# Strassen block products in the down projections of a SwiGLU trunk, with sums of weights on VectorE

## The chip, the cores and the metric

The kernel runs on one core of one Trainium2 chip. Its time is the device time of one execution in microseconds (us), the median of several runs. The engines of a core are TensorE (PE, with its weight loads shown apart as PEld), VectorE (DVE), ScalarE (ACT), GpSimd (POOL) and SyncE (SP, which here issues most DMAs).

## The reference

Two layers of a decoder over a sequence of 256 tokens, width 1024, all in float32. Each layer is a half-step SwiGLU with layer norm, three token mixers side by side with a combined input and an output projection, layer norm, and a second half-step SwiGLU with layer norm. The change concerns the four SwiGLUs (two in each layer):

```python
D_MODEL, SEQ, DEPTH, D_FF = 1024, 256, 2, 2816

def swiglu(x, w_gu, w_down):
    gate, up = jnp.split(x @ w_gu, 2, axis=-1)
    return (jax.nn.silu(gate) * up) @ w_down

def hybrid_layer(x, ...):
    h = layer_norm(DEEPNORM_ALPHA * x + 0.5 * swiglu(x, ffn1_w_gu, ffn1_w_down), ...)
    ...                     # DeltaNet, sliding-window attention, memory attention, merge
    h = layer_norm(DEEPNORM_ALPHA * h + merged @ w_out, ...)
    return layer_norm(DEEPNORM_ALPHA * h + 0.5 * swiglu(h, ffn2_w_gu, ffn2_w_down), ...)
```

A down projection is the product of a 256 x 2816 hidden matrix with a 2816 x 1024 weight matrix.

## The kernel before

**Weights.** All weights come as one stream, `wst`, in tiles of 128x1024 float32 (512 KB), called units here. `unit` does for each: SP's DMA into `raw` (pool `praw`, four buffers), a cast on ACT to a float32r tile `whi` (pool `phi`, five buffers), and on DVE `wlo = raw - whi` (pool `plo`, five buffers; `split` is these two). A `raw` buffer is free when that subtraction is done. Every product is then three matmuls (`mm3`): high part by high part, high by low, low by high, each of 512 columns into a PSUM bank. `newest` is the last split made.

**The gate and up phase.** Hidden tiles come in groups i = 0 to 10, each of four units and 48 matmuls. `out` takes silu times up, transposes on DVE, and sends the result through DRAM with POOL's DMAs (tiles `tr` and `pt`). `settle` splits what came back into `u{i}`, which holds two hidden tiles of 128 rows (by 256 tokens), high and low; it is put off so that the round trip has time, the last two to within the down projection (after units 2 and 10; the table `along`).

**The down projection** is `projA`, called at the end of `Ffn.rest`: NFT = 22 units (unit uu is the weights' row block uu). For a unit there are four blocks: tb = 0, 1 (halves of the tokens) by j = 0, 1 (halves of the 1024 output columns), each an `mm3` into one of four `acc` banks, 12 matmuls a unit. The first two units (`lead`) run with one half of the tokens and then the other. The last units (`tail`, 4 in a layer's first SwiGLU, 6 in its second) are kept to the end and run block by block, so that the residual addition and layer norm of a finished half (`Post`) stand beside the products of the other. The last block of all goes into two half banks (`ends`, from the `at` banks): `Post.early` takes its bank `d` out of the way as soon as the units ahead of the tail are in it.

**Order.** A scheduler sets the order of each engine's instructions from priorities: a unit's load, cast and subtraction get a priority AHEAD = 300 steps earlier than their place in the program. The order is fixed when the kernel is built; each engine works through its own row in that order and waits by semaphores for the others. PSUM has four `acc` banks, two `sm` and two `at`; in the down projection `sm` and `at` are idle before the tail.

Of the kernel before, what the change touches and what calls it, by code (L numbers as in the profile page):

```python
# [17 lines left out]
P = 128  # L18
# [20 lines left out]
def tile_trunk(ctx, tc, x, xT, mem, memT_, wst, lnp, memln, cvw, rows, cst, out):  # L39
# [64 lines left out]
    def unit(w=U, dst=None, cuts=1, behind=None, parts=1):  # L104
# [17 lines left out]
        return hi, lo  # L122

    def split(hi, lo, src):
        return nc.scalar.copy(hi, src).ins, nc.vector.tensor_tensor(lo, src, hi.bitcast(F32), op=ALU.subtract).ins  # L125
# [54 lines left out]

    def projA(xt, w, kpu, nk, outs, tail=0, dsts=(), lead=0, after=None, behind=None, held=(), led=None, along=None, ends=(), units=None):

        def one(k, kk, hi, lo, tb, j):
            ts = slice(tb * P, (tb + 1) * P)
            n = [o.shape[-1] for o in outs[tb]]
            first = k == ((nu - tail) * kpu if tb and j and ends and len(outs[1]) > 2 else 0)
            c = kk * w + sum(n[:j])
            c = slice(c, c + n[j])
            mm3(outs[tb][j], (xt[0](k)[:, ts], xt[1](k)[:, ts]), (hi[:, c], lo[:, c]), first, k == nk - 1 or bool(ends and tb and j and k == (nu - tail) * kpu - 1))

        nu = nk // kpu
        units = units or {}

        def get(uu):
# [34 lines left out]
    def full_rows():  # L229

        a, b, c, d = (acc() for _ in range(4))
        return [[a, b], [c, d]], [at()[:, 0:S] for _ in range(2)]

# [75 lines left out]
    class Ffn:  # L309
        def __init__(self, before=None):  # L310
            self.units = []
            for q in range(KD // 2):
                if before:
                    before(q)
                self.units.append(unit(cuts=2 if before and q == 0 else 1, parts=2 if before and q in (1, 2) else 1))
            self.hu, self.bank, self.due = {}, {}, []

# [29 lines left out]
        def out(self, i, banks):  # L347
# [9 lines left out]
            if len(self.due) > 1:  # L357
                self.settle(act, ins)
            y = T(p2, [P, D], "pt")[:, 0:512]
            d = T(pd, [4, 32, 4, P], "tr")  # L360
# [3 lines left out]
            self.last = act, ins, back  # L364
            self.due.append((i, y))

        def settle(self, act, vec):

            if self.due:
                i, y = self.due.pop(0)  # L370
                hi, lo = (self.h(i)[:, n].rearrange("p a (t q s) -> p (a t) q s", t=2, q=4) for n in range(2))
                with tc.issue_after(act), tc.issue_after(vec):
                    split(hi, lo, y.rearrange("p (q n s) -> p n q s", q=4, n=4))

        def rest(self, hT, tail, dsts, post, mid={}, behind=None, more={}):
            for i in range(1, NFT // 2):
                banks = [acc() for _ in range(2)]
# [14 lines left out]
            outs, ends = full_rows()  # L392
            projA((lambda k: self.hu[k // 2][:, 0, k % 2, :], lambda k: self.hu[k // 2][:, 1, k % 2, :]), D, 1, NFT, outs, tail, dsts, 2, post, along={2: self.settle, 10: self.settle, **more}, ends=ends)

# [809 lines left out]
```

## Time and profile before

| | us |
|---|---|
| median of 3 runs | 1275.11 (1274.64 to 1275.47) |
| span of the profiled execution | 1272.1 |
| down projection, layer 0, first SwiGLU | 126.25 to 183.71, and 2.8 of half-bank matmuls |
| down projection, layer 0, second SwiGLU | 574.04 to about 630 |
| down projection, layer 1, first SwiGLU | 756.24 to about 814 |
| down projection, layer 1, second SwiGLU | 1203.51 to about 1260 |

In the profile's rows the columns are the start (in rows of time), the length in us, the engine, the line, the operation, out<-in, and in square brackets how long the engine sat idle before and what released it. In grouped rows the mean of one is in ns. "SPq" is SP's queue, by which weights are loaded. The times of a DMA are from issue to landing.

### The profile page before, as it was taken

How to read it: one execution, taken by the hardware profiler on the slowest of the kernel's cores; microseconds unless marked ns; L12 is line 12 of the kernel's file. 1: busy time of each engine (PE TensorE's matmuls, PEld its weight loads, DVE VectorE, ACT ScalarE, POOL GpSimd, SP SyncE). 2: the span in 40 equal slices, each digit the busy share in tenths (PEclk: the TensorE clock that was granted, in tenths of full speed). 3: DMA queues.
4: the chain of work that ended last, by engine and by line, in shares of the span. 5: the costliest groups of instructions: out<-in, count | busy, mean ns of one | idle time of the engine just before them, and what ended most of it. 6: DMA issues, size and time to landing. Idle time of an engine off the chain costs nothing.

```text
span 1272.1 us, 18768 instructions
## 1 busy us (share of the span) xinstructions
PE 1260.6 (99%) x6948; PEld 1073.3 (84%) x6948; DVE 864.1 (68%) x1274; ACT 661.4 (52%) x982; POOL 207.2 (16%) x365
## 2 busy tenths in 40 slices
PE   9999999999999999999999999999999999999997
PEld 6888889999778888888888888899987788888886
DVE  6678576886647776665766665759867387766565
ACT  6456444655664544454454554456556554454441
POOL 1232000002311102221012220000023101122100
PEclk9999999999999999999999999999999999999999
DMA  8988765655534748877668877566463356577762
GB/s 294 317 271 289 248 208 159 211 171 129 172 117 144 241 141 259 241 241 220 217 210 244 256 252 219 177 185 213 150 167 134 100 189 225 174 246 244 241 220 82
DMA packets 77643, 261.40 MB, mean 205 GB/s; under 512 B 11920, under 2 KB 13328, under 8 KB 77552
## 3 DMA queue, kind: packets, MB, share of 16 engines
q1 hardware_dynamic: 66320, 232.40, 56.0%
q0 software_dynamic: 11088, 27.68, 8.1%
q8 instruction: 54, 0.88, 0.3%
q14 instruction: 37, 0.30, 0.1%
q10 hardware_dynamic: 144, 0.13, 0.0%
HBM read 246.40 MB, written 13.76 MB: 205 GB/s over the span
## 4 chain that ended last, share of the span: by engine, by line
PE 89%; DMA 3%; POOL 3%; DVE 2%; issue 2%; ACT 0%; SPq 0%; DVEq 0%; POOLq 0%; ACTq 0%
PE acc L134 80%; PE at L134 3%; PE sm L134 2%; DMA w<-dr 2%; PE sm L137 2%; DVE wlo L125 1%; DMA raw<-in_wst_dram 1%; POOL t L808 1%; POOL t L807 1%; PE acc L332 1%; PE acc L333 1%; POOL l L798 1%; PE acc L335 1%; DMA dr<-t 1%; ACT whi L125 0%
## 5 line engine op out<-in xcount | busy, mean ns | idle before, releaser
L125 DVE TENSOR_TENSOR wlo<-raw,whi 128x1024 fp32r<-128x1024 f32 (+2 forms) x405 | 487.0, 1210 | 279.7 <-ACT whi L125 277.5
L125 ACT CAST whi<-raw 128x1024 fp32r<-128x1024 f32 (+2 forms) x405 | 413.7, 1029 | 400.6 <-PE acc L134 316.2
L134 PE MATMUL acc<-whi,hT 128*128 128x512 f32 (+1 forms) x1824 | 562.2, 386 | 0.5 <-ACT whi L125 0.5
L134 PEld LDWEIGHTS acc<-whi,hT 128*128 128x128 f32 x1824 | 340.0, 188 | 69.8 <-ACT whi L125 2.3
L134 PE MATMUL acc<-wlo,hT 128*128 128x512 f32 (+1 forms) x912 | 350.2, 384 | 0.0
L134 PE MATMUL acc<-whi,u 128*128 128x512 f32 x812 | 259.5, 392 | 0.0
L134 PEld LDWEIGHTS acc<-wlo,hT 128*128 128x128 f32 x912 | 171.3, 188 | 33.1 <-DVE wlo L125 1.0
L134 PEld LDWEIGHTS acc<-whi,u 128*128 128x128 f32 x812 | 152.3, 188 | 32.1 <-DVE u L125 0.5
L134 PE MATMUL acc<-wlo,u 128*128 128x512 f32 x406 | 158.2, 390 | 0.0
L362 POOL DMA_DIRECT2D tr<-t x176 | 96.3, 554 | 311.6 <-DVE t L356 303.5
L134 PE MATMUL acc<-hT,whi 128*128 128x256 f32 x672 | 122.2, 284 | 0.0
L134 PEld LDWEIGHTS acc<-hT,whi 128*128 128x128 f32 x672 | 104.6, 192 | 0.0
L134 PE MATMUL acc<-hT,wlo 128*128 128x256 f32 x336 | 95.0, 283 | 0.0
L134 PEld LDWEIGHTS acc<-wlo,u 128*128 128x128 f32 x406 | 76.3, 188 | 15.4
L134 PEld LDWEIGHTS acc<-hT,wlo 128*128 128x128 f32 x336 | 64.3, 191 | 0.0
L363 POOL DMA_DIRECT2D pt<-tr x44 | 25.0, 569 | 192.5 <-DMA tr<-t 138.4
L353 ACT ACTIVATE t<-acc 128x256 f32<-128x256 f32 x88 | 33.5, 381 | 36.9 <-PE acc L134 36.9
L134 PE MATMUL acc<-u,u 128*128 128x512 f32 x186 | 46.4, 394 | 0.0
L354 DVE TENSOR_TENSOR t<-t,acc 128x256 f32<-128x256 f32 x88 | 36.6, 417 | 8.1 <-ACT t L353 4.1
L1000 POOL TENSOR_TENSOR u<-u,gt 128x512 f32<-128x512 f32 x16 | 20.7, 1294 | 125.0 <-DVE gt L998 125.0
L134 PEld LDWEIGHTS acc<-u,u 128*128 128x128 f32 x186 | 34.6, 188 | 7.5
L125 DVE TENSOR_TENSOR u<-pt,u 128x512 fp32r<-128x512 f32 x44 | 28.9, 657 | 9.4 <-ACT u L125 9.4
(236 smaller groups left out, 1165.0 us busy)
## 6 DMA issues: line engine op xcount, KB each, us to landing
raw<-in_wst_dram SPq DMA_DIRECT2D x409, 512.0 KB, 4.4
tr<-t POOLq DMA_DIRECT2D x176, 64.0 KB, 3.8
pt<-tr POOLq DMA_DIRECT2D x44, 256.0 KB, 5.0
raw<-in_wst_dram SPq DMA_DIRECT2D x16, 324.0 KB, 3.0
gB<-in_lnp_dram SPq DMA_DIRECT2D x6, 512.0 KB, 5.8
bB<-in_lnp_dram SPq DMA_DIRECT2D x6, 512.0 KB, 6.2
w<-dr POOLq DMA_DIRECT2D x4, 512.0 KB, 12.0
t<-in_xT_dram SPq DMA_DIRECT2D x4, 256.0 KB, 5.2
```

The lines of the kernel that those rows point to most:

```text
L125: return nc.scalar.copy(hi, src).ins, nc.vector.tensor_tensor(lo, src, hi.bitcast(F32), op=ALU.subtract).ins
L134: return pe(nc.tensor.matmul(*a, **k))
L137: return pe(nc.tensor.transpose(*a))
L332: nc.tensor.matmul(ps, hT[0][:, k, ts], hi[:, c], start=k == 0, stop=False)
L333: nc.tensor.matmul(ps, hT[0][:, k, ts], lo[:, c], start=False, stop=False)
L335: nc.tensor.matmul(ps, hT[1][:, k, ts], hi[:, c], start=False, stop=k == KD - 1)
L353: act = nc.scalar.activation(t[:, :, tb, :], g, AF.Silu).ins
L354: ins = nc.vector.tensor_tensor(t[:, :, tb, :], t[:, :, tb, :], u, op=ALU.mult).ins
L362: nc.gpsimd.dma_start(d[:, :, q].rearrange("b c x -> c b x"), z[32 * q:32 * q + 32].rearrange("c (b x) -> c b x", b=4))
L363: back = nc.gpsimd.dma_start(y, d.rearrange("b c q x -> (b c) (q x)")).ins
L798: nc.gpsimd.tensor_tensor(L32[q, c], AK[c][q, :, 0, q], cs[q, C_LV:C_LV + 32].unsqueeze(1).to_broadcast([32, 4, 32]), op=ALU.mult)
L1000: nc.gpsimd.tensor_tensor(mg[tb][:, js], mg[tb][:, js], gt[tb][:, js], op=ALU.add)
```

## The change

In the down projections every second pair of units becomes a pair by Strassen's scheme (Winograd's variant): a pair of weight tiles is a 2 x 2 block matrix of 128x512 blocks (unit uu gives b11 and b12, unit uu+1 gives b21 and b22), the two hidden tiles by two halves of tokens another. Seven block products replace eight. The pairs begin at units 4, 8, 12, 16 in a layer's first SwiGLU and at 4, 8, 12 in its second.

- `pair_unit` loads two tiles, forms on DVE the float32 sums of weights t3 = b22 − b12, t1 = b12 − b11 (over b12), t2 = t3 + b11, and t4 = b21 − t2 (over b21), and splits eight blocks of 512 columns as seven operands: both tiles (128x1024 each), t2 and t3 together (into one tile `hT` with one buffer), and t4 (into the same tile).
- `settle` forms for the second tile of `pt` the sums of the hidden tiles, four of 128x128, and splits them into a tile out of `homes` (`u13`, `u12`, `u11`, `gt`).
- `Ffn.__call__` issues the seven products, 21 matmuls. Four of them go into banks of their own (`sm`, `at`, `sm`, `at`), which stay open from the first pair to the last; three go straight to `acc` banks.
- `fold` adds the four banks to the residual after the last pair: one copy on ACT and seven operations of 128x512 on DVE.
- `ends` is allocated only after the fold, since its `at` banks are in use until then; bank d closes with the last plain unit ahead of the tail.

```diff
+    def pair_unit():
+        raw = [T(praw, [P, U], "raw") for _ in range(2)]
+        with tc.high_priority(offset=AHEAD):
+            for r in raw:
+                nc.sync.dma_start(r, wst[pos[0]:pos[0] + P * U].rearrange("(p w) -> p w", p=P))
+                pos[0] += P * U
+            (b11, b12), (b21, b22) = ((r[:, 0:512], r[:, 512:U]) for r in raw)
+            sums = T(p2, [P, U], "gt")
+            t2, t3 = sums[:, 0:512], sums[:, 512:U]
+            nc.vector.tensor_tensor(t3, b22, b12, op=ALU.subtract)
+            nc.vector.tensor_tensor(b12, b12, b11, op=ALU.subtract)
+            nc.vector.tensor_tensor(t2, t3, b11, op=ALU.add)
+            parts = [(T(phi, [P, U], "whi", F32R), T(plo, [P, U], "wlo", F32R)) for _ in range(2)]
+            for (hi, lo), r in zip(parts, raw):
+                split(hi, lo, r)
+            nc.vector.tensor_tensor(b21, b21, t2, op=ALU.subtract)
+            more = T(pu, [P, 2, 3, 512], "hT", F32R)
+            flat = more.rearrange("p n m c -> p n (m c)")
+            split(flat[:, 0, 0:U], flat[:, 1, 0:U], sums)
+            newest[:] = split(more[:, 0, 2], more[:, 1, 2], b21)
...
         for uu in range(lead, nu - tail):
-            for tb in range(2):
-                run([uu], tb, range(len(outs[tb])))
+            if uu in pairs:
+                fast(uu, outs)
+            elif uu - 1 not in pairs:
+                for tb in range(2):
+                    run([uu], tb, range(len(outs[tb])))
...
         if ends:
             after.early(outs[1].pop())
-            outs[1] += ends
+            outs[1] += ends()
...
         def settle(self, act, vec):
...
+                    if 2 * i in self.sums:
+                        s = self.sums[2 * i] = T(*self.sums[2 * i])
+                        v = z.rearrange("p (m q s) -> p m q s", m=4, q=4)
+                        for m, a, b, op in ((0, y[:, 1], y[:, 3], ALU.add), (2, y[:, 0], y[:, 1], ALU.subtract), (1, v[:, 0], y[:, 0], ALU.subtract), (3, y[:, 2], v[:, 1], ALU.subtract)):
+                            nc.vector.tensor_tensor(v[:, m], a, b, op=op)
+                        split(s[:, 0], s[:, 1], z.rearrange("p (m t) -> p m t", m=4))
...
+        def __call__(self, uu, outs):
+            if uu == self.pairs[0]:
+                self.side = [sm(), at(), sm(), at()]
+            w = pair_unit()
...
+            p1, p5, p6, p7 = self.side
+            for o, x, name in ((p1, plain(0, 0), "b11"), (p5, summed(0), "t1"), (outs[0][0], plain(1, 0), "b21"), (outs[0][1], summed(3), "b22"),
+                               (p6, summed(1), "t2"), (p7, summed(2), "t3"), (outs[1][0], plain(1, 1), "t4")):
+                own = o in self.side
+                mm3(o, x, w[name], own and first, own and last)
+            if last:
+                self.fold(p1, p5, p6, p7)
+
+        def fold(self, p1, p5, p6, p7):
+            def add(tb, j, v):
+                y = hres[tb][:, j * 512:j * 512 + 512]
+                nc.vector.scalar_tensor_tensor(y, v, 0.5 / ALPHA, y, op0=ALU.mult, op1=ALU.add)
+            u, v = (T(p2, [P, 512], "t2", bufs=4) for _ in range(2))
+            nc.scalar.copy(u, p1)
+            add(0, 0, p1)
+            nc.vector.tensor_tensor(u, u, p6, op=ALU.add)
+            nc.vector.tensor_tensor(v, u, p5, op=ALU.add)
+            nc.vector.tensor_tensor(u, u, p7, op=ALU.add)
+            add(0, 1, v)
+            nc.vector.tensor_tensor(v, u, p5, op=ALU.add)
+            add(1, 0, u)
+            add(1, 1, v)
```

How the order moves. In the rows `wlo` is the low part of a unit, `u10` the last settled hidden tile; numbers are buffers and tiles. First DVE in the middle of layer 0's first down projection. Before, one subtraction for each unit:

```order
L125 TENSOR_TENSOR wlo_263_1346<-raw_261_1344,whi_262_1345 128x1024
L125 TENSOR_TENSOR wlo_266_1364<-raw_264_1362,whi_265_1363 128x1024
L125 TENSOR_TENSOR wlo_269_1384<-raw_267_1382,whi_268_1383 128x1024
L125 TENSOR_TENSOR wlo_272_1402<-raw_270_1400,whi_271_1401 128x1024
L125 TENSOR_TENSOR u10_273_1418<-pt_231_1200,u10_273_1418 128x512
```

After, one round there: the pair of units 12 and 13 (`raw_287`, `raw_288`), then plain unit 14 (`raw_295`) with the split of t4 behind it, then plain unit 15 (`raw_298`):

```order
L134 TENSOR_TENSOR gt_289_1487<-raw_288_1484,raw_287_1483 128x512
L135 TENSOR_TENSOR raw_287_1483<-raw_287_1483 128x512
L136 TENSOR_TENSOR gt_289_1487<-gt_289_1487,raw_287_1483 128x512
L150 TENSOR_TENSOR wlo_291_1492<-raw_287_1483,whi_290_1491 128x1024
L150 TENSOR_TENSOR wlo_293_1494<-raw_288_1484,whi_292_1493 128x1024
L150 TENSOR_TENSOR hT_294_1500<-gt_289_1487,hT_294_1500 128x1024
L140 TENSOR_TENSOR raw_288_1484<-raw_288_1484,gt_289_1487 128x512
L150 TENSOR_TENSOR wlo_297_1528<-raw_295_1526,whi_296_1527 128x1024
L150 TENSOR_TENSOR hT_294_1500<-raw_288_1484,hT_294_1500 128x512
L150 TENSOR_TENSOR wlo_300_1546<-raw_298_1544,whi_299_1545 128x1024
```

Six operations of sums and sums' splits have come between the units' subtractions, and the load of the second tile of the next pair waits for unit 14's (`wlo_297`), which stands eighth. The second down projection of layer 0, after the change, DVE again (a pair, `raw_1069` and `raw_1070`, and the plain unit behind it, `raw_1077`):

```order
L134 TENSOR_TENSOR gt_1071_5794<-raw_1070_5791,raw_1069_5790 128x512
L135 TENSOR_TENSOR raw_1069_5790<-raw_1069_5790 128x512
L136 TENSOR_TENSOR gt_1071_5794<-gt_1071_5794,raw_1069_5790 128x512
L150 TENSOR_TENSOR wlo_1073_5799<-raw_1069_5790,whi_1072_5798 128x1024
L150 TENSOR_TENSOR wlo_1075_5801<-raw_1070_5791,whi_1074_5800 128x1024
L150 TENSOR_TENSOR wlo_1079_5835<-raw_1077_5833,whi_1078_5834 128x1024
L140 TENSOR_TENSOR raw_1070_5791<-raw_1070_5791,gt_1071_5794 128x512
L150 TENSOR_TENSOR hT_1076_5807<-gt_1071_5794,hT_1076_5807 128x1024
L150 TENSOR_TENSOR hT_1076_5807<-raw_1070_5791,hT_1076_5807 128x512
```

Here the plain unit's subtraction comes sixth, ahead of t4 and of the two splits into `hT`. Last the end of layer 0's first down projection on DVE. Before (`h0`, `h1` are the residual's halves; `wlo_329` and on belong to the next stage):

```order
L125 TENSOR_TENSOR wlo_306_1567<-raw_304_1565,whi_305_1566 128x1024
L125 TENSOR_TENSOR wlo_329_1712<-raw_327_1710,whi_328_1711 128x1024
L125 TENSOR_TENSOR wlo_332_1742<-raw_330_1740,whi_331_1741 128x1024
L406 SCALAR_TENSOR_TENSOR h1_222<-acc_236_1210,h1_222 128x512
L125 TENSOR_TENSOR wlo_335_1772<-raw_333_1770,whi_334_1771 128x1024
L418 SCALAR_TENSOR_TENSOR h0_221<-acc_233_1207,h0_221 128x512
```

After (`wlo_322` is the last unit's, `at_255` is p5, `at_257` is p7, `t2_309` and `t2_310` are the fold's u and v, and `wlo_347` and on belong to the next stage):

```order
L150 TENSOR_TENSOR wlo_322_1636<-raw_320_1634,whi_321_1635 128x1024
L445 TENSOR_TENSOR t2_309_1605<-t2_309_1605,at_257_1317 128x512
L438 SCALAR_TENSOR_TENSOR h0_221<-t2_310_1606,h0_221 128x512
L150 TENSOR_TENSOR wlo_347_1783<-raw_345_1781,whi_346_1782 128x1024
L150 TENSOR_TENSOR wlo_350_1813<-raw_348_1811,whi_349_1812 128x1024
L150 TENSOR_TENSOR wlo_353_1843<-raw_351_1841,whi_352_1842 128x1024
L447 TENSOR_TENSOR t2_310_1606<-t2_309_1605,at_255_1315 128x512
L438 SCALAR_TENSOR_TENSOR h1_222<-t2_309_1605,h1_222 128x512
L438 SCALAR_TENSOR_TENSOR h1_222<-t2_310_1606,h1_222 128x512
L496 SCALAR_TENSOR_TENSOR h0_221<-acc_237_1235,h0_221 128x512
```

The last reads of the side banks and the last additions to the residual stand behind three subtractions of the next stage, and the norm's first addition (L496) behind those.

More of the change, by code (lines that the diff above doesn't have):

```diff
@@ L179, in halves, with projA @@
             use(i, b)
-    def projA(xt, w, kpu, nk, outs, tail=0, dsts=(), lead=0, after=None, behind=None, held=(), led=None, along=None, ends=(), units=None):
+    def projA(xt, w, kpu, nk, outs, tail=0, dsts=(), lead=0, after=None, behind=None, held=(), led=None, along=None, ends=None, units=None, fast=None):
         def one(k, kk, hi, lo, tb, j):
@@ L188, in one @@
             c = slice(c, c + n[j])
-            mm3(outs[tb][j], (xt[0](k)[:, ts], xt[1](k)[:, ts]), (hi[:, c], lo[:, c]), first, k == nk - 1 or bool(ends and tb and j and k == (nu - tail) * kpu - 1))
+            mm3(outs[tb][j], (xt[0](k)[:, ts], xt[1](k)[:, ts]), (hi[:, c], lo[:, c]), first, k == nk - 1 or bool(ends and tb and j and k == closing))
         nu = nk // kpu
         units = units or {}
+        pairs = fast.pairs if fast else ()
+        closing = max(u for u in range(nu - tail) if u not in pairs and u - 1 not in pairs) * kpu + kpu - 1
         def get(uu):
@@ L231, in full_rows @@
         a, b, c, d = (acc() for _ in range(4))
[L232 removed]
+        return [[a, b], [c, d]], lambda: [at()[:, 0:S] for _ in range(2)]
     def together(f):
@@ new lines, in pairs @@
+        @property
+        def pairs(self):
+            return tuple(self.sums)
+        def __call__(self, uu, outs):
+            if uu == self.pairs[0]:
+                self.side = [sm(), at(), sm(), at()]
+            w = pair_unit()
+            first, last = uu == self.pairs[0], uu == self.pairs[-1]
+            h, s = self.hu[uu // 2], self.sums[uu]
+            plain = lambda a, t: tuple(h[:, n, a, t * P:(t + 1) * P] for n in range(2))
+            summed = lambda m: tuple(s[:, n, m] for n in range(2))
+            p1, p5, p6, p7 = self.side
[5 more added lines that the diff above has]
+                self.fold(p1, p5, p6, p7)
@@ L375, in rest @@
         def rest(self, hT, tail, dsts, post, mid={}, behind=None, more={}):
+            homes = ((pu, [P, 2, 4, P], "u13", F32R), (pu, [P, 2, 4, P], "u12", F32R), (pu, [P, 2, 4, P], "u11", F32R), (p2, [P, 2, 4, P], "gt", F32R))
+            self.sums = {u: home for u, home in zip(range(4, NFT - tail - 1, 4), homes)}
             for i in range(1, NFT // 2):
```

17 lines of the change are left out of this document (11 added, 6 removed).

## Prediction

> **What bounds the kernel.** I read the page's first rows and the chain by engine, then the four stretches in which the down projections run, and then what a weight tile costs on its way.
>
> ```profile
> PE 1260.6 (99%) x6948; PEld 1073.3 (84%) x6948; DVE 864.1 (68%) x1274; ACT 661.4 (52%) x982; POOL 207.2 (16%) x365
> PE 89%; DMA 3%; POOL 3%; DVE 2%; issue 2%; ACT 0%; SPq 0%; DVEq 0%; POOLq 0%; ACTq 0%
> ```
>
> TensorE is busy for 99% of the span and carries 89% of the chain. By that, each matmul taken away is a gain of its pace, as long as the weights come in time. Over the four down stages the windows say (columns: stretch, its length, busy time of each engine, clock, share of the DMA engines, GB/s):
>
> ```profile
> core 0: us, PE busy (x) PEld busy (x) DVE busy (x) ACT busy (x) POOL busy (x), PEclk, DMA share, GB/s
> 126.25:183.71 57.46, 57.46 (x255) 47.46 (x254) 33.63 (x37) 27.03 (x30) 3.83 (x7) 1.00 0.77 254
> 574.30:630.10 55.80, 55.80 (x248) 46.13 (x247) 34.27 (x40) 25.47 (x28) 2.75 (x5) 1.00 0.74 241
> 756.50:813.70 57.20, 57.20 (x254) 47.23 (x253) 33.18 (x36) 25.67 (x28) 2.75 (x5) 1.00 0.73 234
> 1203.80:1259.60 55.80, 55.80 (x248) 46.14 (x247) 30.67 (x37) 22.21 (x25) 2.97 (x6) 1.00 0.52 175
> ```
>
> In all four PE has not one gap. VectorE (DVE) has some 22 us free in each: that is the cover for the sums, as a total. Whether it is free at the right moment is the question. The pace of a matmul comes from the longest unbroken piece of the chain:
>
> ```profile
> 1094.88 164.68 PE acc L134 x726
> ```
>
> 164.68 / 726 = 0.2268 us. A plain unit (one weight tile, 12 matmuls) is 2.72 us of PE, two units 5.44; a pair of 21 matmuls is 4.76.
>
> How a tile comes in (ScalarE casts, VectorE subtracts, then the tile's `raw` buffer is free and SP sends the next load):
>
> ```profile
> SPq L115 <- DVE wlo L125: 35.4, 16, 4.9
> raw<-in_wst_dram SPq DMA_DIRECT2D x21, 512.0 KB, 4.4
> DMA to landing us min/median/max: 3.9/4.4/6.4
> 140.05 1.05 ACT L125 CAST whi<-raw 128x1024 fp32r<-128x1024 f32 x1 [1.67 <-PE acc L134]
> 142.77 1.05 ACT L125 CAST whi<-raw 128x1024 fp32r<-128x1024 f32 x1 [1.67 <-PE acc L134]
> 141.13 1.23 DVE L125 TENSOR_TENSOR wlo<-raw,whi 128x1024 fp32r<-128x1024 f32 x1 [1.49 <-ACT whi L125]
> 1211.00 3.48 DVE L125 TENSOR_TENSOR wlo<-raw,whi 128x1024 fp32r<-128x1024 f32 x3
> ```
>
> The first row is SP's waits from 128 to 183 us: of 21 loads 16 wait for a subtraction on VectorE, 35.4 us together. So the load of a tile isn't sent ahead at leisure, it is sent when VectorE frees one of the four buffers. Before, that is harmless: landing 4.4 + cast 1.05 + subtraction 1.23 = 6.7 us, and a buffer comes round every 4 × 2.72 = 10.9 us; the casts at 140.05 and 142.77 follow PE's pace and wait for PE.
>
> **The change part by part.**
>
> *Matmuls removed.* 4 pairs in each first FFN and 3 in each second make 14 over two layers, three matmuls less in each: 42 × 0.2268 = **−9.5 us**, if nothing is late.
>
> *Sums on VectorE.* A pair adds four sums of 128x512, the split of t2|t3 (128x1024) and of t4 (128x512); the fold at the end adds seven operations of 128x512.
>
> ```profile
> L500 DVE TENSOR_TENSOR pp<-pp,gB 128x512 f32<-128x512 f32 x4 | 2.8, 692 | 0.1
> L125 DVE TENSOR_TENSOR u<-pt,u 128x512 fp32r<-128x512 f32 x44 | 28.9, 657 | 9.4 <-ACT u L125 9.4
> L125 ACT CAST u<-pt 128x512 fp32r<-128x512 f32 x44 | 27.0, 614 | 11.8 <-DMA pt<-tr 11.8
> L418 DVE SCALAR_TENSOR_TENSOR h<-acc,h 128x512 f32<-128x512 f32 x18 | 12.4, 688 | 13.0 <-PE acc L134 13.0
> L852 DVE TENSOR_TENSOR w<-w,sm 128x128 f32<-128x128 f32 x4 | 1.1, 280 | 1.0 <-PE sm L134 1.0
> ```
>
> 4 × 0.69 + 1.23 + 0.66 = 4.65 us of VectorE a pair, 7 × 0.69 = 4.8 for the fold. In the first down stage that is 33.6 + 4 × 4.65 + 4.8 = 57.0 busy us, against 57.46 − 12 × 0.2268 = 54.7 that PE would need. VectorE alone is over PE there. In the second FFN it is 34.3 + 3 × 4.65 + 4.8 = 53.1 against 55.8 − 9 × 0.2268 = 53.8, just under. ScalarE gets 1.05 + 0.61 a pair and has 30 us free, so it costs nothing while VectorE is the slower. The sums of hidden tiles (for each pair four of 128x128 at 0.28 and a split of 0.66, 1.8 us) stand mostly in the gate and up phase; I take them as hidden by VectorE's idle third there.
>
> *The ring of loads in the first FFNs.* In VectorE's order a pair's eight operations and the next plain unit's subtraction stand in a row, and the load of the next pair's second tile waits for that subtraction. From the landing of the second tile: t3 and t1 1.31 (operations in a row overlap by some 0.07, as the row of three subtractions shows), cast 1.05 (t1 overwrites b12, so it must come first), three subtractions 3.48, t4 0.62, the plain one 1.23, in all 7.7 us; then the next landing. With 4.4 that is a round of 12.1, with the shortest 3.9 one of 11.6. Fewer loads stand in flight at once when the ring is late, so I take 4.1: 11.8. PE needs 4.76 + 5.44 = 10.2 for the round. Each pair after the first makes PE wait **1.6 us**.
>
> The first pair has its own: VectorE comes to it after u9 is settled (its round trip through DRAM lands then).
>
> ```profile
> 126.25 0.39 PE L134 MATMUL acc<-whi,u 128*128 128x512 f32 x1
> 131.65 0.62 ACT L125 CAST u<-pt 128x512 fp32r<-128x512 f32 x1 [3.36 <-DMA pt<-tr]
> 132.30 0.69 DVE L125 TENSOR_TENSOR u<-pt,u 128x512 fp32r<-128x512 f32 x1 [3.22 <-ACT u L125]
> 756.24 0.39 PE L134 MATMUL acc<-whi,u 128*128 128x512 f32 x1
> 759.36 0.62 ACT L125 CAST u<-pt 128x512 fp32r<-128x512 f32 x1 [1.07 <-DMA pt<-tr]
> ```
>
> In layer 0 u9 is done 6.7 us after the stage began; a hidden sum, t3, the split of u8's sums, t1, t2, three subtractions, t4, the plain one, t4's split (0.28 + 0.69 + 0.66 + 1.38 + 0.36 left of the cast + 3.48 + 0.62 + 1.23 + 0.66 = 9.4, less 0.3 for overlaps) end at 15.8. The last two matmuls of the pair read that split, so it ends at 16.3; PE without a wait would end it at 10.9 + 4.76 = 15.65: 0.7 us of wait. In layer 1 u9 comes 2.3 us sooner and nothing waits; the slack left there takes 0.3 off the next pair. Layer 0: 0.7 + 3 × 1.6 = 5.5; layer 1: 1.3 + 2 × 1.6 = 4.5. Together **+10.0**.
>
> *The end of the first FFNs.* Unit 21's load waits for unit 18's subtraction, 7.7 us after the last pair's landing; landed and cast it is ready at 7.7 + 4.1 + 1.05 = 12.9. The pair ends some 8.5 after its landing (t4's split at 8.3 comes last), and PE has 14 matmuls, 3.2 us, before it reads unit 21: a wait of 1.2. Then the half banks of the last block wait for the fold's last read of p5, behind three splits of the next stage: 0.35 more. 1.55 in each of two, **+3.1** (bounds: 0, if the ring isn't late, and 3.9 each, with the longest landing of 6.4).
>
> *Layer norm behind it.*
>
> ```profile
> 183.71 2.83 PE at L134 x24
> 186.54 0.55 PE sm L137 x4
> 187.75 6.39 PE acc L134 x54
> 194.15 0.59 PE sm L137 x4
> 185.64 1.40 DVE L296 SCALAR_TENSOR_TENSOR h<-h,rstd,bB 128x512 f32<-128x512 f32 x2
> ```
>
> PE turns to the first row half's transposes at 186.54, less than 1 us after VectorE began the last operation of that norm (185.64), and to the second half's at 194.15: little slack in each. The residual is now complete only after the fold (4.8 us) and three 1.23 us splits that the order puts ahead of its last additions. Walking it through, the first transposes wait 1.2 us, the second 2.6. Bounds 0 to 3.8; I take 3.0, nearer the upper end since those VectorE operations have nothing beside them that could be left out. **+6.0** for two.
>
> *The second FFNs.* There the plain unit's subtraction stands ahead of t4 and of the two splits, so the next load is asked for 1.31 + 1.05 + 2.4 + 1.23 = 6.0 us after a landing; 6.0 + 4.1 = 10.1 against 10.2: no wait. The settled tiles come early enough:
>
> ```profile
> 574.04 0.39 PE L134 MATMUL acc<-whi,u 128*128 128x512 f32 x1
> 576.83 0.62 ACT L125 CAST u<-pt 128x512 fp32r<-128x512 f32 x1 [0.75 <-DMA pt<-tr]
> ```
>
> 0, with bounds from 0 to 2 us a pair, which a landing of 6.4 instead of 4.1 would give. With six tail units behind the last pair, the fold has 12 × 6 × 0.2268 = 16 us of PE over it.
>
> *Sum:* −9.5 + 10.0 + 3.1 + 6.0 = **+9.6 us**, a span of 1272.1 + 9.6 = 1281.7. The median of the runs, 1275.1, is 3.0 above this span; so about **1285 us**.
>
> **The landing time, by another source.** Eight of the waits (six pairs, two of unit 21) scale with the load's way. The chain has loads that landed faster than the median:
>
> ```profile
> 389.87 3.66 DMA raw<-in_wst_dram
> 1019.32 3.45 DMA raw<-in_wst_dram
> ```
>
> [...]
>
> **The rivals.**
>
> 1. *The loads land sooner.* The ring late means fewer transfers at a time. With 3.45 the eight waits lose 0.65 each, 5.2: +4.4, so 1279.5. Against it: in the first stage no load took under 3.9.
>
> 2. *Only the ring is late.* The tail's and the norm's waits (9.1 us) are covered, since VectorE after a late ring has less left to do and the next stage's splits may be ready early: +0.5, so 1275.6, no change. For it: those terms come from my walk along an order, not from a row.
>
> 3. *All hidden: faster.* The full −9.5, 1265.6 us. One mechanism decides: whether the next pair's second tile is asked for early enough. The round must be at most 10.2, that is 7.7 us of work cut to 6.1 at a 4.1 us landing, or a landing within 2.5. It could come from VectorE operations of 128x512 that overlap more than the rows show, or from casts that run beside the sums. For it: TensorE's 89% of the chain, and 22 us of free VectorE. Against it: 57.0 us of VectorE work against 54.7 of PE.
>
> 4. *The second FFNs are late too.* The margin there is 0.1 us a round. Longer landings add up to 2 us for each of six pairs, less what the first pairs have in hand: some +10, so 1295.
>
> That the change doesn't do what it says is no rival: its order has 42 matmuls fewer on PE.
>
> **How the numbers follow.** The forecast 0.42; rival 1, 0.14; rival 2, 0.16; rival 3, 0.18; rival 4, 0.10. A measurement of this kernel can tell about 0.2%, 2.6 us, from no change: below 1272.5 is faster (rival 3: 0.18), up to 1277.7 the same (rival 2: 0.16), the rest slower (0.66). The range leaves out most of rival 3 and the far part of rival 4: 1268 to 1297. The likeliest case alone has 1281 to 1290, by the bounds of its tail and norm terms.
>
> **What would show it.** In the profile after: PE's busy time falls by about 9.5 us and yet its share of the first FFNs' down stages falls below 90%; PE's idle there is put down to the subtraction of whi or to its cast, once for each pair from the second on, 1 to 2 us each, with a round of some 11.8 us between the pairs' first products; SP's loads wait for VectorE's subtraction of the plain unit; the stretch of the second FFNs has PE without gaps. After the first FFNs' last blocks PE's transposes wait for the norm. If instead the rounds there are 10.2 us, the ring's term is wrong and rival 3 holds; if the rounds are long and the norm on time, rival 2; if the second FFNs show gaps at their pairs, rival 4.

## The result, and the profile after

The changed kernel takes 1291.63 us (median of 4 runs, 1288.22 to 1296.06) where the kernel before takes 1274.99: a ratio of 1.013, 95% interval 1.0108 to 1.0153. It is slower, by 16.6 us; the forecast was 10 us slower, with 1291.63 inside its range. The profiled execution has a span of 1290.7, 18.6 over the one before; the stretches below are those of this one execution.

The page's busy times and the chain by engine, of the changed kernel:

```profile
PE 1264.1 (98%) x6906; PEld 1067.0 (83%) x6906; DVE 957.4 (74%) x1460; ACT 688.7 (53%) x1028; POOL 206.8 (16%) x365
PE 76%; DVE 10%; DMA 8%; issue 3%; ACT 2%; POOL 0%; DVEq 0%; SPq 0%; ACTq 0%; POOLq 0%
```

PE has 42 matmuls fewer and is busy 3.5 us longer; its part of the chain fell from 89% to 76%, and VectorE and the DMAs have 18% of it where they had 5%. (The length of one matmul in the records, 0.39 us, is more than the pace of 0.227, so a gap in PE shows some 0.17 too short, and PE counts as busy while its clock is at half: 3.41 of 3.41 us from 642.40 on, at 0.50.) The four down stages, each from its first down product to its first half-bank product (columns as in the prediction):

```profile
127.05:188.43 61.38, 58.02 (x242) 44.26 (x240) 48.80 (x62) 32.75 (x39) 3.80 (x7) 1.00 0.62 211
581.52:636.74 55.22, 54.40 (x238) 44.40 (x237) 48.93 (x60) 29.79 (x35) 2.88 (x6) 1.00 0.74 233
766.46:827.77 61.31, 57.92 (x242) 44.27 (x240) 48.65 (x61) 31.30 (x37) 2.74 (x5) 1.00 0.57 183
1222.43:1277.95 55.52, 54.47 (x239) 44.31 (x238) 48.01 (x63) 27.02 (x32) 3.28 (x6) 1.00 0.56 177
```

Before, the same stretches took 57.30, 55.88, 57.30 and 55.88 us with PE without a gap. VectorE is not full in the first: 48.8 of 61.4 us. Where PE waited, in all:

```profile
PE sm L159 <- DVE wlo L150: 4.8, 8, 0.8
PE sm L162 <- DVE h L326: 3.8, 2, 1.9
PE acc L159 <- DVE t L384: 1.9, 2, 1.1
PE sm L162 <- issue: 1.8, 1, 1.8
...
PE acc L159 <- DVE hT L150: 1.2, 7, 0.2
```

First row: eight pairs of the first FFNs wait for their first subtraction. Second and fourth: the norms (the fourth, put down to issue, is PE's wait at 206.49 for layer 0's first norm, whose last operation on VectorE had begun at 205.63). Third: the first units of the second FFNs, which no step of the prediction has. From PE's starts in the two timelines, stage by stage (us against before, forecast beside it):

| stretch | forecast | measured |
|---|---|---|
| up to the first down stage | 0 | +0.8 |
| first FFN's down stage, layers 0 and 1 | +4.0, +3.0 | +4.1, +4.0 |
| from there to the second FFN's down stage | +3.35, +3.35 | +2.6, +4.7 |
| second FFN's down stage, layers 0 and 1 | −2.0, −2.0 | −0.7, −0.4 |
| from layer 0's to layer 1's first down stage | 0 | +3.4 |
| sum | +9.6 | +18.6 |

The ring of loads in the first FFN, as the chain tells one round of it (pieces under 0.05 us left out), and the t3 of the round before, from VectorE's timeline:

```profile
164.91 0.69 DVE raw L140
165.59 1.15 DVE wlo L150
166.76 3.73 DMA raw<-in_wst_dram
...
170.58 0.70 DVE gt L134
171.31 0.70 DVE raw L135
...
172.08 1.06 ACT whi L150
173.16 2.36 DVE wlo L150 x2
```
```profile
158.92 0.69 DVE L134 TENSOR_TENSOR gt<-raw,raw 128x512 f32<-128x512 f32 x1 [1.20 <-DMA raw<-in_wst_dram]
```

The chain's pieces are t4, the plain unit's subtraction, the load that it lets go (3.73 us), t3, t1, the cast and the subtractions. The round before began with t3 at 158.92, this one at 170.58: 11.66 us, forecast 11.8. The request in between left at 166.76, 7.84 us after t3 began.

Layer 0's second norm, in the chain, VectorE's and PE's timelines, and windows around it:

```profile
633.56 6.45 DMA bB<-in_lnp_dram
```
```profile
640.12 1.42 DVE L326 SCALAR_TENSOR_TENSOR h<-h,rstd,bB 128x512 f32<-128x512 f32 x2 [1.44 <-DMA bB<-in_lnp_dram]
640.93 0.66 PE L162 MATMUL sm<-cs,h 128*128 128x128 f32 x4 [1.89 <-DVE h L326]
```
```profile
636.00:641.90 5.90, 4.01 (x30) 3.63 (x29) 4.32 (x11) 0.57 (x2) 0.00 (x0) 1.00 0.39 142
641.90:645.30 3.40, 3.40 (x21) 3.40 (x19) 2.87 (x8) 1.49 (x3) 0.00 (x0) 0.57 0.00 0
```

The norm's bias row left SP's queue at 633.56, behind six weight loads of the next stage that wait for VectorE, and landed at 640.0; VectorE was ready 1.44 us before. PE waited 1.89 us, and the granted clock then averaged 0.57 over the last window (0.50 from 642.40 to 645.81 us, as the last section shows): some 1.7 us more.

### The profile page after: what moved, and what is told of

It reads as the page before. It is cut to its first block, busy times and chain, and to the rows that moved or that the text cites. A ratio compares the mean times of both kernels' runs of the same rounds, so it can differ in the third digit from the quotient of the medians.

```text
span 1290.7 us, 18905 instructions
## 1 busy us (share of the span) xinstructions
PE 1264.1 (98%) x6906; PEld 1067.0 (83%) x6906; DVE 957.4 (74%) x1460; ACT 688.7 (53%) x1028; POOL 206.8 (16%) x365
## 4 chain that ended last, share of the span: by engine, by line
PE 76%; DVE 10%; DMA 8%; issue 3%; ACT 2%; POOL 0%; DVEq 0%; SPq 0%; ACTq 0%; POOLq 0%
PE acc L159 65%; DMA raw<-in_wst_dram 5%; DVE wlo L150 5%; PE at L159 4%; PE sm L159 3%; ACT whi L150 2%; PE sm L162 1%; DMA pt<-tr 1%; DMA tr<-t 1%; PE acc L362 1%; PE acc L363 1%; PE acc L365 1%; PE at L162 1%; DVE u L150 1%; DVE hT L150 1%
## 5 line engine op out<-in xcount | busy, mean ns | idle before, releaser
L159 PE MATMUL acc<-whi,u 128*128 128x512 f32 x640 | 212.3, 394 | 1.9 <-DVE t L384 1.9
L159 PEld LDWEIGHTS acc<-whi,u 128*128 128x128 f32 x640 | 120.0, 188 | 29.4 <-issue 2.7
L159 PE MATMUL acc<-wlo,u 128*128 128x512 f32 x320 | 125.1, 391 | 0.0
L159 PEld LDWEIGHTS acc<-wlo,u 128*128 128x128 f32 x320 | 60.1, 188 | 12.9 <-DVE wlo L150 0.7
L150 DVE TENSOR_TENSOR u<-pt,u 128x512 fp32r<-128x512 f32 x56 | 37.1, 663 | 7.8 <-ACT u L150 7.8
L384 DVE TENSOR_TENSOR t<-t,acc 128x256 f32<-128x256 f32 x88 | 36.7, 417 | 7.8 <-ACT t L383 4.2
```

The source lines that it names most:

```text
L159: return pe(nc.tensor.matmul(*a, **k))
L384: ins = nc.vector.tensor_tensor(t[:, :, tb, :], t[:, :, tb, :], u, op=ALU.mult).ins
```

## The experiments

Each ratio is to the kernel before, timed beside the run. Stages are given against before, in the order: first FFNs (layers 0 and 1), the stretches behind them, second FFNs, the stretch behind layer 0's. They come from one profiled execution each, which can lie some us from the run's median; where it lies over 2 us away, the text says so.

**Which FFNs.** Pairs in the second FFNs alone, and in the first alone:

```diff
-            self.sums = {u: home for u, home in zip(range(4, NFT - tail - 1, 4), homes)}
+            self.sums = {u: home for u, home in zip(range(4, NFT - tail - 1, 4), homes) if tail == 6}
```

> Pairs only in the two second FFNs (tail 6); the first FFNs run plain units as before. Theory (each stage carries its own loss): by the trace of the changed kernel against before, the second FFNs' down stages give -0.66 and -0.36 us and layer 0's norm behind them +3.4 (1.9 us of PE waiting for the norm and a stretch at half clock behind it): 1275.0 + 2.4 = about 1277.5. Rival (the losses come from VectorE's load over the whole kernel, or from the first FFNs' lateness handed on): without the first FFNs' pairs the second ones' norm isn't late, 1275.0 - 1.0 to -4 = 1271 to 1274.

Measured 1277.03 us, ratio 1.0013 (1.0004 to 1.0022): as the first theory had it. Six pairs in the second FFNs alone are a small loss: −0.1 and −0.6 in their stages, +4.0 in layer 0's norm, where PE waits 2.5 us and the clock falls as above (0.50 from 636.0 to 638.6).

> Pairs only in the two first FFNs (tail 4); the second FFNs run plain units. Theory (stage by stage): +0.8 before the first down stage, +4.1 and +4.0 in the two down stages, +3.0 and +4.4 in the norms behind them: 1275.0 + 16.3 = about 1291. Rival (second FFNs carry part of it): 1285 or less.

 (Here `tail == 4` stands in the edit.)

Measured 1287.79, ratio 1.0108 (1.0089 to 1.0127): between the two numbers. The profiled stages are +2.6 and +2.1, the stretches behind them +2.5 and +3.4, in an execution of 1284.58 us, 3.2 under the median. They are below the changed kernel's +4.1 and +4.0 mainly at the first pair (in layer 1 at the first two); in layer 0 its t3 begins 2.2 us sooner here, at 132.95 for 135.15. The two parts together, 2.7 + 13.5 us, make up 16.2 of the 16.6 of the whole change. Up to the first down stage this run has +0.06 with the sums of hidden tiles in it and the run before +0.89 without any: the +0.8 of the changed kernel there is not the sums' cost.

**The order in the round.** The plain unit is fetched between the pair's splits and t4 (`...` marks what is left out):

```diff
-    def pair_unit():
+    def pair_unit(between):
...
+        between()
+        with tc.high_priority(offset=AHEAD), tc.issue_after(newest[1]):
             nc.vector.tensor_tensor(b21, b21, t2, op=ALU.subtract)
...
-                fast(uu, outs)
+                fast(uu, outs, lambda: get(uu + 2))
```

> In each pair the next plain unit's load, cast and subtraction are written ahead of t4 and the sums' splits, which have to follow that subtraction on VectorE: the first FFNs get the order that the second ones have already. Theory (the ring of loads: the next second tile is asked for 7.7 us after the last one landed; now 6.0): the round falls from 11.7 to about 10.2, six rounds 1.5 shorter, 9 us less: about 1282.5, with the norms' waits as they were. Rival (VectorE's sum of work, 57 us in a stage of 55, is what counts, not its order): the wait moves to the products of t2 and t4, which come later now, and the time stays within 3 us of 1291.6.

Measured 1282.23, ratio 1.0062 (1.0050 to 1.0074). The total came as forecast by the theory, its parts did not. The rounds fell to 10.3 to 11.2 us (from t3 to t3), less far than to 10.2, and the middle pairs' waits to 0.5 us or less, as the ring says; but PE's waits now are

```profile
PE acc L161 <- DVE wlo L152: 2.7, 5, 0.8
PE acc L161 <- ACT hT L152: 2.3, 2, 1.7
PE sm L161 <- DVE hT L152: 2.0, 4, 1.2
```

in layer 0 for the first pair and the fourth, in layer 1 above all for the fourth and its products of sums, so the down stages gained only 1.0 and 1.7 us (+3.1, +2.3). The rest came behind them: less lateness for the norms (+2.3, +1.4), no stretch at half clock (0.999 over the span, where the changed kernel has 0.996), and PE waits 0.4 instead of 1.9 us for layer 0's second norm.

**The norm's rows.** First their loads on GpSimd's queue, then (in a kernel with pairs in the second FFNs alone) with the weights' priority on SP's:

```diff
-        load(gB, gap.partition_broadcast(P))
-        load(bB, bap.partition_broadcast(P))
+        nc.gpsimd.dma_start(gB, gap.partition_broadcast(P))
+        nc.gpsimd.dma_start(bB, bap.partition_broadcast(P))
```

> The loads of the norms' gain and bias rows (gB, bB) go out on GpSimd's queue instead of SP's, nothing else. Theory (in layer 0's second FFN bB stands on SP's queue behind weight loads that wait for VectorE; it lands at 640.0, 1.4 us after VectorE is ready for it, PE waits 1.9 us, and the clock then drops to half for 3.4 us): that place gets its 3.4 us back, 1288. Rival (the norm is late by VectorE's order, the load only lands in its shadow): within 1 us of 1291.6, with PE waiting at the same place for the norm.

Measured 1291.99, ratio 1.0136 (1.0123 to 1.0149): no gain. At the place itself the edit did what it should, PE's wait there fell from 1.9 to 0.6 us. But every norm's rows moved, and in the profile PE waits 2.9 us for the first cast at the start and 1.6 us in layer 1's merge that weren't there. The time was lost again elsewhere, and whether the theory holds needs the cleaner edit:

```diff
-                self.gb = gb(*self.aps)
+                with tc.high_priority(offset=AHEAD):
+                    self.gb = gb(*self.aps)
```

> Pairs only in the second FFNs, and the norms' rows gB and bB loaded with the weights' priority, so that they stand ahead of the next stage's weight loads on SP's queue. Theory (the second FFN's norm is late by bB's load alone, and the half clock follows from that wait): the wait of 2.5 us at layer 0's second norm and the 1.7 us lost at half clock go: 1277.0 - 3.5 = about 1273.5. Rival (VectorE's order makes the norm late): the wait stays, 1276 to 1277.

Measured 1273.74, ratio 0.9991 (0.9983 to 1.0000): 3.3 us under the same kernel without the edit. PE's wait for the norm went from the first row to the second,

```profile
PE sm L162 <- DVE h L326: 2.5, 1, 2.5
```
```profile
PE sm L162 <- DVE h L326: 0.3, 1, 0.3
```

and the clock stayed at 1.00 there (0.999 over the span, for 0.997). The same edit without pairs:

> The kernel before with the norms' rows gB and bB loaded with the weights' priority, no pairs. Theory (before, bB lands in time, so this load is only a cost of the change): 1274.6, no difference over 0.1%. Rival (part of what the norm's loads gave in the run with pairs in the second FFNs is a gain of its own): 1 us or more under the kernel before.

Measured 1274.58, ratio 1.0000 (0.9991 to 1.0008). So the late bias row was a cost of the change, by way of SP's queue.

**The bank of the last gate and up group.** In the changed kernel's second FFN VectorE's timeline has

```profile
580.35 0.69 DVE L134 TENSOR_TENSOR gt<-raw,raw 128x512 f32<-128x512 f32 x1 [1.72 <-DMA raw<-in_wst_dram]
...
583.42 0.42 DVE L384 TENSOR_TENSOR t<-t,acc 128x256 f32<-128x256 f32 x1
...
586.02 0.42 DVE L384 TENSOR_TENSOR t<-t,acc 128x256 f32<-128x256 f32 x1
```

The first pair's sum waits 1.7 us for its tile, and behind it stands the product (L384) that frees PE's bank. PE waits 0.8 us for it.

```diff
-                ins = nc.vector.tensor_tensor(t[:, :, tb, :], t[:, :, tb, :], u, op=ALU.mult).ins
+                self.mult = ins = nc.vector.tensor_tensor(t[:, :, tb, :], t[:, :, tb, :], u, op=ALU.mult).ins
...
-            w = pair_unit()
+            with tc.issue_after(self.mult):
+                w = pair_unit()
```

> As the run before, and on VectorE the first pair's sums have to follow the last gate and up group's product (before, the sums' wait for their weight tile stood ahead of it and held PE's bank). Theory: the 1.0 us that PE waits for that bank in each of the two stages goes too: about 1271.5, 0.2% under the kernel before. Rival (the pair then comes later and PE waits there instead): no gain on the run before.

Measured 1275.18, ratio 0.9999 (0.9990 to 1.0009). The wait for the bank is gone from the trace (the stage of layer 0 is at −1.5, layer 1's at +0.1), yet nothing is gained: PE waits 1.2 us for layer 0's norm (0.3 in the run before) and 0.6 for a split of a tail tile in layer 1, and 1.5 in layer 1's merge, which lies ahead of that stage. The rival was right on the sum, not on the place: PE waits for no pair. Why the merge waits, here and in the run with the rows on GpSimd's queue, these runs don't show.

**Three pairs, four pairs, and the fold.** The plain unit, the norms' rows (on SP's queue) and the bank edited as above, with the fold under the weights' priority; the first run has pairs at 4, 8 and 12 everywhere, the second keeps the first FFNs' fourth:

```diff
-                self.fold(p1, p5, p6, p7)
+                with tc.high_priority(offset=AHEAD):
+                    self.fold(p1, p5, p6, p7)
```

> Three pairs in each of the four FFNs (4, 8, 12), the plain unit's subtraction ahead of t4 and the splits, gB and bB with the weights' priority, the last group's product ahead of the first pair's sums, the fold with the weights' priority. 36 matmuls fewer, -8.2 us if nothing waits. Theory (each loss is a place in an order, and the last pair of the first FFNs was the worst of them): remaining waits of 2 to 4 us, mostly in the first FFNs' first pair: 1268 to 1271. Rival (VectorE's work in the first FFNs is too much in any order): 1275 or more.

> The same with the fourth pair in the first FFNs kept (4, 8, 12, 16). Theory: the fourth pair's own waits (its split of t4 comes late, and the tail's first units behind it) and the norm right behind the fold stay, 2 to 3 us for each first FFN: 1273 to 1276, above the run with three pairs by 3 to 6 us. Rival (with the order mended four pairs are as good as three): 1.4 us under it.

Measured 1282.22 (1.0054, 1.0037 to 1.0071) and 1289.54 (1.0113, 1.0092 to 1.0134): both far over, the second by 7.3 us more than the first (its profiled execution, of 1284.74 us, lies 4.8 under its median). In the run with three pairs the first FFNs are at last −1.8 each; but the second ones are +4.7 and +4.9, from one wait in each, of 4.5 and 3.7 us, and the half clock (0.50) that follows for 3.4 and 6.8 us (0.994 over the span):

```profile
PE acc L161 <- DVE u L152: 8.3, 2, 4.5
```

Its cause stands in VectorE's timeline. The fold has eight operations on VectorE (four sums of banks, four additions to the residual), one more than the text on the change says. From 614.69 on the last seven of them and two splits of later tail units (at 618.60 and 620.34, units 20 and 21 by the order of loads and casts) run ahead of the tail tile's split (at 621.47) that PE needs:

```profile
614.69 0.68 DVE L447 TENSOR_TENSOR t<-t,sm 128x512 f32<-128x512 f32 x1
...
616.80 1.28 DVE L442 SCALAR_TENSOR_TENSOR h<-t,h 128x512 f32<-128x512 f32 x2
...
620.34 1.22 DVE L152 TENSOR_TENSOR wlo<-raw,whi 128x1024 fp32r<-128x1024 f32 x1
621.47 1.22 DVE L152 TENSOR_TENSOR u<-raw,u 128x1024 fp32r<-128x1024 f32 x1
```

Without the fold's priority and without the bank's edit, both at once:

> The run with three pairs without two of its edits: the fold has no priority of its own, and nothing holds the first pair's sums behind the last group's product. Theory (what went wrong there was the fold, which stood on VectorE ahead of splits of tail units in the second FFNs: PE waited 4.6 and 3.7 us for one of them): the second FFNs' down stages come back from +4.7 and +4.9 to -0.5 to -1.0, the first ones keep -1.8 each, the norms +2 and +0.8: about 1274.5, the kernel before within 0.2%. Rival (three pairs everywhere keep VectorE too busy in the second FFNs): above 1278.

Measured 1271.08 us, ratio 0.9967 (0.9957 to 0.9978): **faster than both kernels**, by 0.3% than the one before. In VectorE's row the tail tile's split now begins at 617.07, ahead of the fold's last four operations, and PE no longer waits for it; so of the two edits taken out it is the fold's priority that the trace shows to matter there. Its profiled stages: first FFNs −1.5 and −1.2, behind them +1.0 and +0.1, second −0.4 and −0.7, behind layer 0's +0.1, and +0.8 up to the first down stage. The first down stage has no gap in PE any more, in 55.8 us:

```profile
127.03:182.82 55.79, 55.79 (x245) 45.52 (x243) 49.26 (x61) 31.44 (x36) 3.13 (x6) 1.00 0.80 270
```

and of 36 × 0.2268 = 8.2 us that the matmuls save some 3 are kept. Last, the changed kernel with only the fourth pair left out:

```diff
-            self.sums = {u: home for u, home in zip(range(4, NFT - tail - 1, 4), homes)}
+            self.sums = {u: home for u, home in zip((4, 8, 12), homes)}
```

> The changed kernel with the fourth pair of the first FFNs left out, and nothing else edited (gB and bB as in the changed kernel). In the order built so, the plain unit's subtraction stands ahead of t4 and the sums' splits in the first FFNs too, without an edit for it. Theory (the first FFNs' loss comes from that order and from the fourth pair, whose lateness meets the tail; the second ones' from bB): the first FFNs' down stages at -1 to -1.5, the norms behind them +1, layer 0's second norm still +3 by bB: 1276 to 1278, some 14 us under the changed kernel and 5 over the run with three pairs and the norm's rows ahead. Rival (the order had to be written ahead by hand): the rounds of the first FFNs stay near 11.7 us, 1283 or more.

Measured 1273.14, ratio 0.9988 (0.9976 to 1.0000), 3 us better than forecast: the first FFNs at −0.9 and +0.1, behind them +0.4 and +0.3, layer 0's second norm +1.9 by bB still (the profiled execution, of 1275.62 us, lies 2.5 over the median). Leaving the two fourth pairs out takes 18.5 us off the changed kernel: they save 1.4 us of PE and cost 20. Part goes with the pair in any order (the run with the plain unit ahead, which has it, is 9.1 us over this one, and four pairs were 7.3 us over three under all edits), part is the order: with three pairs the scheduler puts the plain subtraction ahead by itself, and the first FFNs' last rounds are 10.1 to 10.2 us long.

The fourth pair also delays the first, at the other end of the stage. Its hidden sums stand ahead of the first pair's on VectorE, and they take one of the two `gt` buffers in which every pair forms t2 and t3. In the changed kernel the first pair's t3 (second row) stands behind the split of u9 (first row), for which VectorE sat idle 4.31 us; with three pairs (last row) it stands ahead of it:

```profile
134.34 0.69 DVE L150 TENSOR_TENSOR u<-pt,u 128x512 fp32r<-128x512 f32 x1 [4.31 <-ACT u L150]
...
135.15 0.68 DVE L134 TENSOR_TENSOR gt<-raw,raw 128x512 f32<-128x512 f32 x1
```
```profile
126.65 0.69 DVE L134 TENSOR_TENSOR gt<-raw,raw 128x512 f32<-128x512 f32 x1 [1.78 <-DMA raw<-in_wst_dram]
```

With three pairs in this order no pair makes PE wait, the first included. What in the fourth pair costs most, its place right ahead of the tail, its hidden sums, the buffer or its 4.65 us of VectorE work, the runs don't tell apart: none has three pairs with one of them at 16.

**VectorE's total, or its way.** Three of the four sums of weights on GpSimd:

```diff
-            nc.vector.tensor_tensor(t3, b22, b12, op=ALU.subtract)
+            nc.gpsimd.tensor_tensor(t3, b22, b12, op=ALU.subtract)
...                                               (t2 and t4 alike)
```

> The changed kernel with three of a pair's four sums of weights (t3, t2, t4) on GpSimd, which does a sum of 128x512 in 1.3 us where VectorE takes 0.7. VectorE has 2.1 us less to do for each pair. Theory (the ring of loads, that is the way from a landing to the plain unit's subtraction, not VectorE's total): the way gets longer, t3 1.3 + t1 0.7 + t2 1.3 in a row ahead of the casts and subtractions, 8 to 8.5 us to the plain one for 7.7, so the rounds are 11.9 to 12.5 us and the time is 1290 to 1296. Rival (VectorE's total of 57 us in a stage of 55): 2.1 x 14 less work on the bound engine brings back 8 us or more, 1283 or less.

Measured 1310.70, ratio 1.0288 (1.0258 to 1.0317): 19 us slower than the changed kernel, with less work on VectorE (947.0 us busy for 957.4). The rival falls: less VectorE work brought nothing back. The rounds are 12.8 to 13.3 us from the second pair on, over the forecast 11.9 to 12.5, as the way from a landing to the next request got longer: t3 and t2 take 1.30 and 1.79 us one after the other (at 160.36 and 161.74), and in this kernel's order the split of the two stands ahead of the pair's own subtractions, with VectorE idle 2.26 us for its cast (up to 164.64). So the order differs too, not the engine of the sums alone. t4's 2.1 us (first row) hold up its own product, not the request:

```profile
L140 POOL TENSOR_TENSOR raw<-raw,gt 128x512 f32<-128x512 f32 x14 | 29.2, 2085 | 47.5 <-DVE wlo L150 27.6 <-issue 19.8
L136 POOL TENSOR_TENSOR gt<-gt,raw 128x512 f32<-128x512 f32 x14 | 23.3, 1663 | 0.8
L134 POOL TENSOR_TENSOR gt<-raw,raw 128x512 f32<-128x512 f32 x14 | 19.2, 1368 | 35.0 <-DMA raw<-in_wst_dram 31.1 <-DMA tr<-t 3.7
```

## Why the prediction was right, and where it was not

*The ring of loads.* Right in its mechanism: SP's request for the next pair's second tile waits for the plain unit's subtraction, and a round took 11.66 us for 11.8. Its two parts were off in opposite ways: the load took 3.73 us for 4.1, and the way from t3 to the request 7.84 for 7.7. The sizes of the stages, +4.1 and +4.0 for +4.0 and +3.0, are in part luck. By PE's starts against its pace the four pairs lost 2.0, 1.4, 1.1 and 1.3 us in layer 0 (forecast 0.7 and three times 1.6) and 1.2, 2.2, 1.3 and 1.2 in layer 1 (forecast 0, 1.3, 1.6 and 1.6), and the tails 0.5 and 0.4 (forecast 1.2 each). The step "nothing waits" at layer 1's first pair failed. And the same two stages cost only +2.6 and +2.1 in the profile of the run with pairs in the first FFNs alone. In the five first-FFN rounds that the chain passes through, the load from SP's queue took 3.66 to 3.73 us in four and 4.45 in the fifth, against the 4.1 of the walk and the 3.45 of rival 1.

*Two signs that did not come.* PE's busy time rose by 3.5 us where it was to fall by 9.5, and its share of the first FFNs' down stages is 94.5%, not below 90%. Both were read from busy records, which hide part of each short gap (some 0.17 us); the length of the stages shows the loss.

*VectorE's sum of work.* It was named as the reason against rival 3. It is not the bound: where 57.0 us had been added up, 48.8 of 61.4 us are busy, and that though the fold has eight operations and not the seven of the sum. Taking sums off VectorE made the kernel slower, while an order with the same work made it 9 us faster.

*The end of the first FFNs and the norm behind.* The forecast of 3.35 each met 2.6 and 4.7. The walk had two waits for the norm in each layer; the trace has one, of 1.84 and 1.89 us, for the second half's transposes, and the first half's stand later in PE's order (200.19) and don't wait. The 4.7 holds a stretch at half clock (847.20 to 850.61) that no term had.

*The second FFNs, "no waits".* This step failed. The ring there is on time, as forecast (no pair waits); but the sums in VectorE's row delay the last group's product, by 0.8 to 1.1 us of PE, and the stages gave 0.7 and 0.4 of their 2.0.

*What hides the fold there.* "16 us of PE over it" is true of the fold and forgot the norm's rows: on SP's queue bB stands behind weight loads that wait for a busier VectorE. That is 3.4 us, shown by the run that moves it ahead, and the largest single miss. This step and the one before make 6.4 of the 9 us between +9.6 and +18.6. The rest is 1.1 in the first FFNs' stages, 0.6 behind them and 0.8 ahead of the first down stage, whose cause is open.

*The fourth pair.* It had no term of its own. With it left out and nothing else edited the loss is gone, so it, in the order that it brings, and not the scheme, makes the change a loss. Its own products wait (in the run with the plain unit ahead PE lost 1.9 and 3.0 us there), and it holds up the first pair's start.

## What to carry to other kernels

Saved matmuls count only where the next weights are asked for in time: follow one buffer from its landing, through every operation in the order of its engine, to the request that it frees, and compare that round with PE's; the engine's busy share (VectorE 74% here) doesn't tell. Then ask what else stands on the same queue behind a request that now waits, such as the norm's two rows (spread over the partitions, 512 KB each). And price the last special unit by itself, at both ends of the stage: what it needs early stands ahead of the others, and what it leaves late has little plain work behind it.

## What was not expected of the hardware

**Half clock after a wait of under 2 us.** Two waits of the changed kernel in PE's timeline (the first rows; the one before 640.93 is shown above), windows around the wait before 206.49 (second rows), and windows around the one before 640.93 (third rows):

```profile
206.49 1.33 PE L162 MATMUL sm<-cs,h 128*128 128x128 f32 x8 [1.84 <-issue]
845.88 1.29 PE L162 MATMUL sm<-cs,h 128*128 128x128 f32 x8 [1.89 <-DVE h L326]
```
```profile
202.08:205.49 3.41, 2.57 (x20) 2.14 (x19) 3.41 (x9) 1.74 (x4) 0.00 (x0) 1.00 0.00 0
205.49:208.91 3.42, 1.92 (x11) 1.42 (x12) 3.38 (x6) 1.18 (x2) 0.00 (x0) 1.00 0.00 0
```
```profile
638.99:642.40 3.41, 1.52 (x14) 1.48 (x14) 2.25 (x4) 0.59 (x1) 0.00 (x0) 1.00 0.03 11
642.40:645.81 3.41, 3.41 (x18) 3.31 (x17) 2.92 (x8) 1.69 (x2) 0.00 (x0) 0.50 0.00 0
```

Waits of nearly the same length left the clock at 1.00 at 206.49 and brought it to 0.50 at the other two places (642.40 to 645.81 and 847.20 to 850.61). What differs is where they fall. In the changed kernel's profile both stretches at half clock inside the work last 3.413 us, and they begin 186 and 246 times 3.413 us after the clock first rose to 1.00 (at 7.52 us). Laid on the grid that this gives, the waits before 640.93 and 845.88 fall whole into one window, which leaves PE 1.89 and 1.95 us idle there, and the wait before 206.49 is cut in two by a boundary, with 0.84 and 1.50 us idle in the two windows. That the clock goes by the idling within such a window is the author's estimate from these three places. In the run with four pairs under all edits a longer wait, of 1.91 us before 1260.04, left the matmuls behind it at 0.39 to 0.40 us; so the length of a wait alone doesn't decide. The four runs of the changed kernel spread over 8 us; the kernel before lay within 1 us in the four beside them, but from 1273.22 to 1279.72 us in later rounds, so how much of the spread is half clock stays open.

**GpSimd's sums beside VectorE.** The same sum of 128x512 took 1.37, 1.66 or 2.09 us on GpSimd in the mean, by its line, and VectorE's split of the sums took longer in that kernel (second row) than in the changed one (first):

```profile
L150 DVE TENSOR_TENSOR hT<-gt,hT 128x1024 fp32r<-128x1024 f32 x14 | 17.1, 1219 | 0.0
```
```profile
L150 DVE TENSOR_TENSOR hT<-gt,hT 128x1024 fp32r<-128x1024 f32 x14 | 21.5, 1533 | 13.6 <-ACT hT L150 13.6
```

One by one, the sums with no VectorE operation beside them took 1.30 to 1.32 us (1.30 at 160.36), and the t4 sums with VectorE at work beside them 2.13 to 2.15 (2.14 at 155.09). The sums with VectorE beside a part of them took 1.73 to 1.81 (1.79 at 161.74). Of VectorE's fourteen splits ten took 1.21 to 1.23 us and four, each with a GpSimd sum beside it, 2.31. A few that overlapped were not slowed (four sums took 1.30 to 1.34, two splits 1.22), so overlap alone does not decide; what the two engines share isn't shown by these runs.
